# Seven block products in four instead of three of the eight K pairs of the gate and up matmuls

## The chip, the cores and the metric

The kernel runs on one core of a Trainium2 chip. The metric is the device time in microseconds (us) of one execution. Before the change its median over three runs is 2574.28 us (2572.94 to 2577.58).

## What is computed

A two-layer decoder trunk on 256 tokens of width 2048, in float32: layer 0 mixes with a state-space scan, layer 1 with differential attention, and each is followed by a SwiGLU feed-forward network (FFN) between RMSNorms. The change touches the FFN only:

```python
D_MODEL = 2048; SEQ = 256; D_FF = 5632; DEPTH = 2
def swiglu(h, w_gate, w_up, w_down):
    return (jax.nn.silu(h @ w_gate) * (h @ w_up)) @ w_down
...
for i in range(DEPTH):
    h = rmsnorm(x, norm_mix_pre[i])
    m = ssd_mixer(...) if i % 2 == 0 else diff_attention(...)
    x = x + rmsnorm(m, norm_mix_post[i])
    h = rmsnorm(x, norm_ffn_pre[i])
    x = x + rmsnorm(swiglu(h, ...), norm_ffn_post[i])
```

## The kernel before

**Numbers.** Every float32 matmul is done as three matmuls in TensorE's rounded type (float32r): an operand is split into a rounded part `hi` and a remainder `lo`, and hi·hi, hi·lo and lo·hi are summed in PSUM. The weights come from HBM as float32 into a tile `raw` of 128x4x512 (three buffers). `prep` (L112 to L126) makes `hi` on ScalarE (L119, a cast) and `lo` on VectorE (L120, raw minus hi). The `hi` and the `lo` tiles have four buffers each; a tile is given back when TensorE has used it. The activations lie transposed and split in `xT`.

**The FFN.** `ffn` works on 512-column chunks, 11 of gate and up. Chunk 10 goes through `mv` (eight ordinary products); the other ten go in five pairs through `pair` (L206 to L267), first gate, then up, so `pair` is called ten times in an FFN and twenty times in the kernel. The order is cut into three parts: chunks (10, 0, 1), then (2, 3, 4, 5), then (6, 7, 8, 9); behind each part `out_proj` multiplies what there is by w_down. So one part holds a gate and an up call, two parts hold gate, up, gate, up.

**One call of `pair`.** It multiplies two token tiles (t = 0, 1) by two column chunks over K = 2048. K is cut into eight pairs `kp` of two 128-row tiles, so that each `kp` is a product of a 2x2 block matrix (tokens by K halves) with a 2x2 block matrix (K halves by chunks). Two kinds of `kp` exist:

- an ordinary one (called R below): eight block products, 24 matmuls of 128x128 by 128x512, one `prep` of the four raw blocks (2048 elements per partition);
- one in `SEVEN` (called S below): seven block products, 21 matmuls, after the Winograd form of Strassen's scheme. A DMA on GpSimd's queue adds one weight block to another in SBUF (L233). `prep` of blocks 1 to 3 (1536 elements per partition) comes first; then VectorE makes three sums of weight blocks in place (L247 to L249, each reading what the one before wrote); then a second `prep` takes all four blocks (2048 elements). Four of the seven products (`p1`, `p5`, `p6`, `p7`) go to PSUM tiles `cp` that are summed over all S of the call and combined on VectorE at the last one (L263 to L267); the other three go straight to the accumulators `acc`.

An S also needs four sums of the activations of its K pair, the token forms. `make_form` (L754 to L768) computes them once per FFN and per S: six VectorE operations, a cast on ScalarE and a subtraction on VectorE, written to a tile `ff`. The first of them is put one step into the up product of chunk 10 and each next three steps later (`later(1 + 3 * k, ...)`, L804).

**The residual's places.** The tag `xr` has four buffers (L718). Outside the FFN's middle they hold the residual, two tiles for each token tile. Before the forms are made, the residual is written to DRAM (L802); before the last `out_proj` of the FFN it is fetched back (`fetch_x`, L721 to L728). In between the forms lie in those buffers: three of the four.

**Order.** The code emits a call `kp` by `kp`. Tile's planner makes one fixed order of instructions for each engine from it, and every engine works in that order; the `raw` loads go on SyncE's queue, the adding DMAs on GpSimd's. When the call's last `kp` is through, VectorE combines the accumulators with the saved products (L778 for gate, L787 and L788 for up), and for up the product is transposed by TensorE (L278) and split (L271 on ScalarE, L272 on VectorE).

Of the kernel before, what the change touches and what calls it, by code (L numbers as in the profile page):

```python
# [29 lines left out]
LAG = 4  # L30
LAG2 = 2

SEVEN = (2, 4, 6)


@with_exitstack
def trunk_kernel(ctx, tc, x_rows, x_cols, vec_cols, vec64, post_rows, lam_rows,
# [103 lines left out]
    def later(k, fn):  # L141
        at = step_no[0] + k
        i = len(deferred)
        while i and deferred[i - 1][0] > at:
            i -= 1
        deferred.insert(i, (at, fn))
# [592 lines left out]
    def ffn(wg, wu, wd, step, final):  # L739
# [14 lines left out]
        def make_form(kp):  # L754

            n, k = kp // 2, kp % 2 * 2
            xf = t512("xf", (P, NT, 2, P))
            f = t512("f", (P, 4, P))
            for t in range(NT):
                sl = slice(t * P, (t + 1) * P)  # L760
                nc.vector.tensor_tensor(xf[:, t], xT_hi[n][:, k:k + 2, sl].bitcast(F32),
                                        xT_lo[n][:, k:k + 2, sl].bitcast(F32), op=ALU.add)
            nc.vector.tensor_tensor(f[:, 0], xf[:, 1, 0], xf[:, 1, 1], op=ALU.subtract)
            nc.vector.tensor_tensor(f[:, 1], xf[:, 1, 0], xf[:, 0, 0], op=ALU.subtract)
            nc.vector.tensor_tensor(f[:, 2], xf[:, 0, 0], f[:, 0], op=ALU.subtract)
            nc.vector.tensor_tensor(f[:, 3], xf[:, 0, 1], f[:, 2], op=ALU.subtract)
            ff = forms[kp] = xr_tile("ff", (P, 4, 2, P), F32R)
            split(ff[:, :, 0], ff[:, :, 1], f)  # L768
# [5 lines left out]
        def g_done(p):  # L774
            def done(t, c, ps, ss):
                g, op = ss[(t, c)]
                gt[(t, 2 * p + 1 - c)] = g
                nc.vector.tensor_tensor(g, ps, g, op=op)  # L778
                nc.scalar.activation(g, g, AF.Silu, scale=rs(t))
            return done  # L780

        def u_done(p):
            def done(t, c, ps, ss):
                ch = 2 * p + 1 - c
                g = gt[(t, ch)]
                y, op = ss[(t, c)]
                nc.vector.tensor_tensor(y, ps, y, op=op)  # L787
                nc.vector.scalar_tensor_tensor(g, y, rs(t), g, op0=ALU.mult, op1=ALU.mult)  # L788

                def piece():  # L790
                    acts[(t, ch)] = act_piece(g, f"f{step}_{ch}_{t}")
                later(2, piece)
            return done

        def twos(w, c):
            return [[w[c + e, kp // 2, :, kp % 2 * 2:kp % 2 * 2 + 2] for e in range(2)] for kp in range(8)]

        mv([wg[10, k] for k in range(4)], u_stat, g_evac, LAG)
        for t in range(NT):
            rs(t)  # L800
            for h in range(2):
                nc.sync.dma_start(xr_d[t][h].rearrange("p (e k) -> p e k", e=2), xr_of[(t, h)])  # L802
        for k, kp in enumerate(SEVEN):
            later(1 + 3 * k, lambda kp=kp: make_form(kp))  # L804
        mv([wu[10, k] for k in range(4)], u_stat, u_evac, LAG2)
        parts = [(10, 0, 1), (2, 3, 4, 5), (6, 7, 8, 9)]
        for pi, part in enumerate(parts):
            for c in part:
                if c < 10 and c % 2 == 0:
                    pair(twos(wg, c), SEVEN, form, g_done(c // 2))  # L810
                    pair(twos(wu, c), SEVEN, form, u_done(c // 2))
            last = pi == len(parts) - 1
# [190 lines left out]
```

## Time and profile before

| | |
|---|---|
| median of 3 runs | 2574.28 us |
| the profiled execution | 2578.97 us, of it 2577.2 us span |
| TensorE granted clock | 0.997 |
| matmuls of `pair` (L224) | 3660, of 11922 in all |
| HBM read | 499.44 MB, 196 GB/s over the span |
| adding DMAs (L233) | 60 of 256 KB |

A row of a timeline gives the start, the duration, engine, line and operation, with how often it follows itself; in square brackets stands the idle time before it and what ended that. [...]

### The profile page before, as it was taken

The page shows a single profiled execution, that of the slowest core. Times are in us where ns is not written, and L with a number is a line of the kernel's source. Part 1 is how long each engine was busy: PE and PEld are TensorE (multiplying, and loading weights), DVE is VectorE, ACT ScalarE, POOL GpSimd, SP SyncE. Part 2 cuts the span into 40 slices and gives each one's busy share as a digit, 9 for nine tenths or more (in the row PEclk, how much of TensorE's full clock was granted, in tenths as well). Part 3 has the DMA queues.
Part 4 walks back from the last instruction along what each step waited for, and adds up shares of the span by engine and source line. Part 5 has one row for each costly group of instructions (what it writes and reads, how often), then busy time and mean ns, then how long its engine had stood idle before and what let it go on. Part 6 is the DMA issues. An engine that isn't in the chain of part 4 may idle for free.

```text
span 2577.2 us, 30784 instructions
## 1 busy us (share of the span) xinstructions
PE 2546.3 (99%) x11922; PEld 2082.6 (81%) x11922; DVE 1796.5 (70%) x2056; ACT 1335.3 (52%) x1628; POOL 204.5 (8%) x176
## 2 busy tenths in 40 slices
PE   8999999999999999999999999999999999999998
PEld 7877888788878888888888778887788888888886
DVE  8777547676677668856885665556578488758874
ACT  4676545665565454534454554445555455435542
POOL 2021000120100000000001000001100000000001
PEclk9999999999999999999999999999999999999999
DMA  6645555454756566666666544544566566656663
GB/s 222 205 166 188 180 193 196 167 180 164 269 200 212 212 198 210 210 215 197 205 235 229 190 147 164 170 157 143 211 198 228 199 208 206 224 194 206 208 243 132
DMA packets 120337, 507.80 MB, mean 197 GB/s; under 512 B 11840, under 2 KB 28544, under 8 KB 84352
## 3 DMA queue, kind: packets, MB, share of 16 engines
q1 hardware_dynamic: 110896, 489.27, 54.6%
q0 software_dynamic: 8640, 15.73, 3.8%
q8 instruction: 93, 1.52, 0.2%
q10 hardware_dynamic: 656, 0.85, 0.1%
q14 instruction: 52, 0.43, 0.1%
HBM read 499.44 MB, written 6.36 MB: 196 GB/s over the span
## 4 chain that ended last, share of the span: by engine, by line
PE 84%; DVE 7%; issue 4%; ACT 3%; DMA 3%; POOL 0%; DVEq 0%; SPq 0%; ACTq 0%; POOLq 0%
PE acc L173 49%; PE acc L224 19%; PE acc L198 5%; PE cp L224 5%; DVE lo L120 3%; PE acc L200 2%; ACT hi L119 2%; DMA raw<-in_w_u_dram 1%; PE sc L879 1%; DMA raw<-in_w_d_dram 1%; PE py L534 1%; PE pt_f L278 1%; DMA mt<-acum_d 1%; PE ptx L615 0%; PE pc L441 0%
## 5 line engine op out<-in xcount | busy, mean ns | idle before, releaser
L120 DVE TENSOR_TENSOR lo<-raw,hi 128x2048 fp32r<-128x2048 f32 (+2 forms) x548 | 1064.7, 1959 | 571.6 <-ACT hi L119 562.3
L119 ACT CAST hi<-raw 128x2048 fp32r<-128x2048 f32 (+2 forms) x548 | 877.1, 1612 | 877.0 <-PE acc L173 295.1
L173 PE MATMUL acc<-hi,xT 128*128 128x512 f32 x1792 | 591.5, 401 | 2.3 <-ACT xT L620 2.0
L224 PE MATMUL acc<-hi,xT 128*128 128x512 f32 x1840 | 589.1, 390 | 0.0
L224 PEld LDWEIGHTS acc<-hi,xT 128*128 128x128 f32 x1840 | 345.3, 188 | 71.2
L173 PEld LDWEIGHTS acc<-hi,xT 128*128 128x128 f32 x1792 | 337.0, 189 | 78.1 <-issue 5.9
L224 PE MATMUL acc<-lo,xT 128*128 128x512 f32 x920 | 358.1, 389 | 0.0
L173 PE MATMUL acc<-lo,xT 128*128 128x512 f32 x896 | 353.1, 394 | 1.6 <-DVE lo L120 1.6
L173 PE MATMUL acc<-hi,ah_f 128*128 128x512 f32 x704 | 274.5, 391 | 0.0
L173 PE MATMUL acc<-lo,ah_f 128*128 128x512 f32 x704 | 274.5, 390 | 0.0
L173 PE MATMUL acc<-hi,al_f 128*128 128x512 f32 x704 | 274.4, 390 | 0.0
L224 PEld LDWEIGHTS acc<-lo,xT 128*128 128x128 f32 x920 | 172.7, 188 | 36.2 <-DVE lo L120 0.4
L173 PEld LDWEIGHTS acc<-lo,xT 128*128 128x128 f32 x896 | 169.4, 189 | 38.4 <-issue 3.9
L198 PE MATMUL acc<-xT,hi 128*128 128x512 f32 x512 | 180.4, 398 | 0.0
L173 PEld LDWEIGHTS acc<-hi,al_f 128*128 128x128 f32 x704 | 132.2, 188 | 27.2
L173 PEld LDWEIGHTS acc<-lo,ah_f 128*128 128x128 f32 x704 | 132.2, 188 | 27.0 <-DVE lo L120 0.2
L173 PEld LDWEIGHTS acc<-hi,ah_f 128*128 128x128 f32 x704 | 132.2, 188 | 26.9
L200 PE MATMUL acc<-xT,lo 128*128 128x256 f32 x512 | 142.9, 280 | 0.0
L124 DVE SCALAR_TENSOR_TENSOR lo<-raw,cols,hi 128x512 fp32r<-128x512 f32 x128 | 92.6, 772 | 53.1 <-ACT hi L123 52.8
L224 PE MATMUL cp<-hi,ff 128*128 128x512 f32 x360 | 120.8, 390 | 0.0
L198 PEld LDWEIGHTS acc<-xT,hi 128*128 128x128 f32 x512 | 96.1, 188 | 23.0
L123 ACT ACTIVATE hi<-raw,cols 128x512 fp32r<-128x512 f32 x128 | 84.6, 715 | 53.1 <-PE acc L173 37.8
(247 smaller groups left out, 2844.1 us busy)
## 6 DMA issues: line engine op xcount, KB each, us to landing
raw<-in_w_d_dram SPq DMA_DIRECT2D x88, 1024.0 KB, 4.9
raw<-in_w_zxbc_dram SPq DMA_DIRECT2D x80, 1024.0 KB, 4.8
raw<-in_w_g_dram SPq DMA_DIRECT2D x160, 512.0 KB, 4.9
raw<-in_w_u_dram SPq DMA_DIRECT2D x160, 512.0 KB, 5.5
raw<-in_w_qkv_dram SPq DMA_DIRECT2D x48, 1024.0 KB, 4.8
raw<-in_w_so_dram SPq DMA_DIRECT2D x32, 1024.0 KB, 4.9
raw<-in_w_ao_dram SPq DMA_DIRECT2D x16, 1024.0 KB, 5.2
mt<-acum_d SPq DMA_DIRECT2D x16, 512.0 KB, 7.0
```

The source lines that it names most:

```text
L119: nc.scalar.copy(hi, raw)
L120: nc.vector.tensor_tensor(lo, raw, hi.bitcast(F32), op=ALU.subtract)
L123: nc.scalar.activation(hi[:, j], raw[:, j], AF.Copy, scale=scale[j])
L124: nc.vector.scalar_tensor_tensor(lo[:, j], raw[:, j], scale[j], hi[:, j].bitcast(F32), op0=ALU.mult, op1=ALU.subtract)
L173: nc.tensor.matmul(acc[t], a, b[:, j], start=(i == 0 and j == 0 and q == 0), stop=(i == last and j == 1 and q == 2))
L198: nc.tensor.matmul(acc[ct], hi[:, j, cs], x.rearrange("p a s -> p (a s)"), start=(i == 0 and j == 0), stop=False)
L200: nc.tensor.matmul(acc[ct][:, :S], lo[:, j, cs], x[:, 0], start=False, stop=(i == last and j == 1))
L224: nc.tensor.matmul(acc[k], a, b, start=first and q == 0, stop=last and q == 2)
L278: nc.tensor.transpose(pt[:, j], src[:, j * P:(j + 1) * P], ident)
L534: nc.tensor.matmul(py[e * 64:(e + 1) * 64, a], xd[c][:, 2 * a + e], mts[c][:, 2 * a + e], start=True, stop=True)
L879: nc.tensor.matmul(sc[c][:, h], qT[cp, h, ts], kT[cp, h, :nk * P], start=True, stop=True)
```

## The change

`SEVEN` names four K pairs instead of three, and other ones. `last` in `pair` stays K pair 6. A fourth form is made, at step 10, and the forms fill all four buffers of the tag `xr`.

```diff
-SEVEN = (2, 4, 6)
+SEVEN = (1, 3, 4, 6)
```

What reads it:

```python
for k, kp in enumerate(SEVEN):
    later(1 + 3 * k, lambda kp=kp: make_form(kp))
...
pair(twos(wg, c), SEVEN, form, g_done(c // 2))
pair(twos(wu, c), SEVEN, form, u_done(c // 2))
```

In a call the order of kinds was R R S R S R S R and is now R S R S S R S R.

## The prediction

> **What bounds the kernel now.** I read the page first, then the rows of one product tile on TensorE, then VectorE's timeline in a stretch of `pair`.
>
> ```profile
> span 2577.2 us, 30784 instructions
> PE   2546.3 (99%) x11922; PEld 2082.6 (81%) x11922; DVE 1796.5 (70%) x2056; ACT 1335.3 (52%) x1628; POOL 204.5 (8%) x176
> ```
> ```profile
> 776.55 0.39 PE L224 MATMUL cp<-hi,xT 128*128 128x512 f32 x1
> 786.75 0.39 PE L224 MATMUL cp<-hi,xT 128*128 128x512 f32 x1
> ```
>
> By the page TensorE (PE) is the bound and VectorE (DVE) has 30% to spare. Both numbers need care. The two rows are the first matmuls of K pair 2 and K pair 4 of one call: between them lie an S (21 matmuls) and an R (24), so 45 matmuls in 10.20 us, 0.2267 us each, not the 0.39 us that a row shows. An S costs TensorE 4.76 us, an R 5.44.
>
> The 70% is a mean over the whole kernel. In `pair` it is another matter. Here is VectorE in a gate call (all S work of it up to the combining, R means an L120 of 2048):
>
> ```profile
> 1264.10 1.75 DVE L120 TENSOR_TENSOR lo<-raw,hi 128x1536 fp32r<-128x1536 f32 x1
> 1265.89 0.69 DVE L247 TENSOR_TENSOR raw<-raw 128x512 f32<-128x512 f32 x1
> 1266.61 0.69 DVE L248 TENSOR_TENSOR raw<-raw 128x512 f32<-128x512 f32 x1
> 1267.22 0.68 DVE L249 TENSOR_TENSOR raw<-raw 128x512 f32<-128x512 f32 x1
> ...
> 1276.12 0.69 DVE L247 TENSOR_TENSOR raw<-raw 128x512 f32<-128x512 f32 x1
> ...
> 1286.45 0.69 DVE L247 TENSOR_TENSOR raw<-raw 128x512 f32<-128x512 f32 x1
> ...
> 1290.58 4.49 DVE L120 TENSOR_TENSOR lo<-raw,hi 128x2048 fp32r<-128x2048 f32 x2 [2.11 <-ACT hi L119]
> ```
> ```profile
> ACT hi L119 <- DVE raw L249: 224.7, 56, 5.8
> ```
>
> One S on VectorE is: `lo` of three blocks, three sums, then 2.11 us of nothing, then `lo` of four blocks. The hole is a dependency: ScalarE (ACT) can cast the sums only when the third is done, and VectorE can subtract only what is cast. The wait table has ScalarE waiting for L249 in 56 of the 60 S of the kernel, so almost no S is without it. From one L247 to the next is 10.33 us (1276.12 to 1286.45), an S and an R. Two `lo` of 2048 take 4.49 us, the first 2.29, so an R costs 2.20 and an S 8.13. TensorE does the same two in 10.20: VectorE's chain, holes included, is the slower one already.
>
> The rest of VectorE's work in a call is the combining. Two stretches, each with one R inside:
>
> ```profile
> 1210.10 0.68 DVE L264 TENSOR_TENSOR su<-cp,s 128x512 f32<-128x512 f32 x1
> 1214.08 2.28 DVE L120 TENSOR_TENSOR lo<-raw,hi 128x2048 fp32r<-128x2048 f32 x1
> 1217.48 1.75 DVE L120 TENSOR_TENSOR lo<-raw,hi 128x1536 fp32r<-128x1536 f32 x1
> ...
> 1251.58 0.68 DVE L264 TENSOR_TENSOR su<-cp,s 128x512 f32<-128x512 f32 x1
> 1260.70 2.28 DVE L120 TENSOR_TENSOR lo<-raw,hi 128x2048 fp32r<-128x2048 f32 x1
> ```
>
> After gate it takes 1217.48 − 1210.10 − 2.20 = 5.18 us, after up 1264.10 − 1251.58 − 2.20 = 10.32. So VectorE's chain is, for gate, 3 × 8.13 + 5 × 2.20 + 5.18 = 40.57 us, for up 45.71, together 86.28. TensorE's is 2 × 183 × 0.2267 = 82.97. From the first S to the last S of a part with four calls the chain gives 86.28 + 40.57 + (2 S and 2 R) 20.66 = 147.51 us. The first and the last `cp` of the two such parts of layer 0, and of the short part:
>
> ```profile
> L224 PE MATMUL cp<-hi,xT x24: 389/389/389, 926.6 to 1074.1; 128*128 128x512 f32 x24
> ```
> ```profile
> L224 PE MATMUL cp<-hi,xT x24: 389/389/389, 1185.3 to 1332.7; 128*128 128x512 f32 x24
> ```
> ```profile
> L224 PE MATMUL cp<-hi,xT x12: 389/389/389, 776.5 to 838.9; 128*128 128x512 f32 x12
> ```
>
> 147.5 and 147.4: TensorE and VectorE are level here, and TensorE hardly waits:
>
> ```profile
> PEld cp L224 <- DVE lo L120: 0.7, 3, 0.3
> ```
>
> That is in the stretch 1258 to 1301. TensorE is the bound by a hair, with VectorE on its heels.
>
> **The change, step by step.** *Removed:* three matmuls in each of 20 calls, 60 × 0.2267 = 13.6 us of TensorE, 0.5%. A call becomes 180 matmuls, 40.8 us.
>
> *Added on VectorE and ScalarE:* in each call one R becomes an S, 8.13 in place of 2.20 on VectorE's chain, +5.93 us (3.8 busy, 2.1 hole). On ScalarE a cast of three blocks more, which has room at 52%. The chain becomes 4 × 8.13 + 4 × 2.20 + 5.18 = 46.50 for gate, 51.64 for up, 98.1 for both, against 81.6 on TensorE. VectorE's chain is now the bound by far, and the saved matmuls are worth nothing there.
>
> How far can VectorE run ahead? Its lead is limited by the four `hi` tiles, which TensorE gives back. At one S of a call that starts level:
>
> ```profile
> 1203.30 6.88 DVE L120 TENSOR_TENSOR lo<-raw,hi 128x2048 fp32r<-128x2048 f32 x3 [2.11 <-ACT hi L119]
> ```
> ```profile
> 1205.69 0.39 PE L224 MATMUL cp<-hi,xT 128*128 128x512 f32 x1
> ```
>
> The sums' `lo` ends at 1203.30 + 2.29 = 1205.6, and TensorE needs it nine matmuls into the S, at 1207.7: 2.1 us of slack, once at the start of each part.
>
> Now the parts. From the first to the last `cp`, K pair 1 of the first call to K pair 6 of the last: in a part of two calls 46.50 + (3 S and 2 R) 28.79 = 75.3, in a part of four 98.14 + 46.50 + 28.79 = 173.4. Ahead of the first S there is one R less than before (−5.44); behind the last nothing changes. So a short part gains 75.3 − 62.4 − 5.4 − 2.1 = +5.4 us, a long one 173.4 − 147.5 − 5.4 − 2.1 = +18.4. Two FFNs with one short and two long each: 2 × (5.4 + 36.8) = +84 us.
>
> *What may fill holes:* four S in 20 calls make 80 holes of 2.11 us. Where the planner's fixed order puts combining work or the next cast between L249 and the second `lo`, a hole costs nothing. Bounds: none filled, 0; all filled, more than the whole loss. In before it fills hardly any (the wait row above), and where VectorE is tightest ScalarE stands still ahead of the sums' cast:
>
> ```profile
> 1267.98 5.10 ACT L119 CAST hi<-raw 128x2048 fp32r<-128x2048 f32 x3 [5.28 <-issue]
> ```
>
> Three casts in a row start here, the sums' first; the two behind it are of the next two K pairs and need no sums, yet none was put into the 5.28 us. I stay near that row. But the first S now comes right behind K pair 0, where the combining falls, so I let a quarter of 20 such holes be filled, −10 us. Sum: **+74 us**.
>
> *At nothing:* two more forms. One form is, from
>
> ```profile
> L761 DVE TENSOR_TENSOR xf<-xT x12: 416/419/423, 738.1 to 1881.3; 128x256 f32<-128x256 f32 x12
> L763 DVE TENSOR_TENSOR f<-xf x6: 285/292/294, 738.9 to 1884.6; 128x128 f32<-128x128 f32 x6
> L272 DVE TENSOR_TENSOR ff<-f,ff x6: 681/685/689, 742.2 to 1888.9; 128x512 fp32r<-128x512 f32 x6
> ```
>
> 2 × 0.42 + 4 × 0.29 + 0.69 = 2.7 us of VectorE. Cover is chunk 10's up product, where each K pair is an R and VectorE has holes such as
>
> ```profile
> 758.69 2.29 DVE L120 TENSOR_TENSOR lo<-raw,hi 128x2048 fp32r<-128x2048 f32 x1 [2.55 <-ACT hi L119]
> ```
>
> Uncovered, two would cost 5.4; nothing else of the change makes it less, so 0 to 5.4. The residual's first fetch found a free place and went early; now all four wait on SyncE's queue for forms, with weight loads behind them:
>
> ```profile
> SPq L725 <- PE cp L224: 3.3, 4, 1.1
> ```
>
> One more such wait per FFN is up to 1.1 us each, and the residual is needed only behind the last `out_proj`: 0 to 2.2, I take 0. K pairs 3 and 4 are neighbours, and an S holds its `raw` tile longest: load, adding DMA, sums, cast, `lo`.
>
> ```profile
> raw<-in_w_u_dram SPq DMA_DIRECT2D x160, 512.0 KB, 5.5
> raw<-in_w_u_dram POOLq DMA_DIRECT2D x30, 256.0 KB, 4.1
> ```
>
> With three tiles, the tile of K pair 3 is reloaded for 6, then for the next call's 1 and 4. From one release to the next takes 5.5 + 4.1 + three sums 2.0 + hole 2.1 + `lo` 2.2 = 15.9 us (GpSimd's issue apart). The chain above gives 2 × 8.13 + 2.20 = 18.5 for the same three K pairs, so the loads are covered, with 2.6 us to spare; their price is 0 here and comes up only if the chain is quicker.
>
> **The rivals.**
>
> *A, VectorE's chain binds in full* (the sum above): +45 to +100 us, about 2619 to 2674, chance 0.60.
>
> *B, the planner fills part of the holes.* In a chain that is behind, TensorE gives tiles back early, and the next K pair's cast could go ahead of the sums' cast. For: with K pairs 3 and 4 next to each other there is a cast of three blocks to put there. Against: it did not happen in before where VectorE was tight. With half of its 15 holes filled a long part has 15 × 1.05 us less, +2.6, and a short one is back at TensorE's bound, −6 × 0.2267 = −1.4: 4 × 2.6 − 2 × 1.4 = +8 in all. So +5 to +45, about 2579 to 2619, chance 0.17; within 5 us of before, chance 0.06. Here the three `raw` tiles would be next: a run of S in one tile, 3 to 6 to 1 to 4, is 3 × 15.9 = 47.7 for nine K pairs, in which TensorE needs 45.6.
>
> *C, TensorE stays the bound: faster.* If the holes are hidden, only busy time counts. In six calls of before VectorE is busy
>
> ```profile
> sum 251.10, PE 251.10 PEld 207.54 DVE 204.25 ACT 128.75 POOL 13.94; mean PE 41.85 PEld 34.59 DVE 34.04 ACT 21.46 POOL 2.32
> ```
>
> 34.04 of 41.85 us a call; 3.8 more are 37.9, below 40.8. Then the 13.6 us come in whole: 2560.7. It decides where more than about six in ten holes are filled. Chance 0.17. [...]
>
> **How the numbers follow.** The profiled execution took 2578.97 us, 0.2% over the median; the sum is a difference and I add it to the median: 2574.3 + 74 = 2648. About 0.2% (5 us) is what a measurement can tell from no change. Faster by more than that: C, 0.17. Within: 0.06. Slower: A and B, 0.77. The range leaves out C and what lies above A's end (few per cent): 2570 to 2675; A's own range is 2619 to 2674.
>
> **What would show it.** Right: 3600 matmuls on L224 with the same 0.2267 us between starts, waits of L224 for L120 that grow from a microsecond to some 70; 80 waits of about 2.1 us ahead of a 2048 `lo`; two L247 some 8.1 us apart in each call (K pairs 3 and 4); from first to last `cp` about 171 us in a long part, 73 in a short one. The step on the chain is wrong if L120's of 2048 follow L249 without a hole. Wrong altogether: a long part near 149 us from `cp` to `cp`, which is TensorE's bound there (3 × 40.8 + 25.2 = 147.6 of matmuls, and the transposes). If L247 waits for the adding DMA, the tiles of `raw` are what I priced too low.

## The result and the profile after

The changed kernel takes 2678.84 us (median of 4 runs, 2670.16 to 2682.77) against 2573.62 us of the kernel before on the same chip: ratio 1.0395 (95% interval 1.0383 to 1.0407), +105 us. The forecast was +74, with 2675 as the upper end: the direction was right, and the loss is larger than the range allowed. The profiled execution took 2681.9 us, 2680.1 of it span, at a granted clock of 0.987 (before 0.997).

The page of after, span and engines:

```profile
span 2680.1 us, 30843 instructions
PE 2581.8 (96%) x11862; PEld 2081.9 (78%) x11862; DVE 1871.1 (70%) x2150; ACT 1360.1 (51%) x1650; POOL 222.6 (8%) x196
```

VectorE has 75 us more to do, but its share of the span is 70%, as before. No share of this page shows what is wrong. VectorE's timeline in an up call of after does; its first two rows are the last of the gate call's combining and the first `lo` of K pair 1, the L247 are the first sums of K pairs 1, 3, 4 and 6:

```profile
1249.06 0.68 DVE L778 TENSOR_TENSOR sx<-acc,sx 128x512 f32<-128x512 f32 x1
1249.66 1.75 DVE L120 TENSOR_TENSOR lo<-raw,hi 128x1536 fp32r<-128x1536 f32 x1
1252.52 0.69 DVE L247 TENSOR_TENSOR raw<-raw 128x512 f32<-128x512 f32 x1 [1.11 <-DMA raw<-in_w_u_dram]
...
1262.85 0.69 DVE L247 TENSOR_TENSOR raw<-raw 128x512 f32<-128x512 f32 x1
...
1264.18 0.69 DVE L249 TENSOR_TENSOR raw<-raw 128x512 f32<-128x512 f32 x1
1266.97 3.96 DVE L120 TENSOR_TENSOR lo<-raw,hi 128x2048 fp32r<-128x2048 f32 x2 [2.11 <-ACT hi L119]
1270.97 0.69 DVE L247 TENSOR_TENSOR raw<-raw 128x512 f32<-128x512 f32 x1
...
1281.29 0.69 DVE L247 TENSOR_TENSOR raw<-raw 128x512 f32<-128x512 f32 x1
```

K pairs 3 and 4 stand 8.12 us apart (forecast 8.13), an S and an R 10.32 (forecast 10.33), and the 2.11 us hole is there. From the table of waits of after:

```profile
ACT hi L119 <- DVE raw L249: 352.5, 72, 6.6
PE cp L224 <- ACT hi L119: 47.6, 28, 3.4
PE acc L224 <- ACT hi L119: 19.2, 40, 0.6
DVE raw L247 <- DMA raw<-in_w_u_dram: 20.4, 12, 4.0
```

The columns are total us, times, longest. ScalarE now waits for the third sum in 72 of 80 S; in VectorE's timeline of the whole kernel the hole behind it is 2.0 to 2.1 us long in 79 of the 80. And L224 waits 47.6 + 19.2 = 66.8 us (forecast some 70, though named for L120; it is the cast, L119, that the first product with summed blocks lacks). The last line is what the forecast had priced at nothing: the first sum waits 20.4 us for the adding DMA; in before that wait is

```profile
DVE raw L247 <- DMA raw<-in_w_u_dram: 1.9, 3, 1.1
```

From the first to the last `cp`, the short part and the two long parts of layer 0 of after:

```profile
L224 PE MATMUL cp<-hi,xT x16: 389/389/389, 772.9 to 850.0; 128*128 128x512 f32 x16
```
```profile
L224 PE MATMUL cp<-hi,xT x32: 389/389/393, 933.4 to 1106.6; 128*128 128x512 f32 x32
```
```profile
L224 PE MATMUL cp<-hi,xT x32: 389/389/393, 1212.1 to 1388.3; 128*128 128x512 f32 x32
```

77.1, 173.2 and 176.2 us, where the forecast had 73 and 171; in layer 1 they are 74.4, 172.0 and 172.3. All but 2 us of the loss of the two profiled executions (101.3 of 103.0) lies in the six parts that call `pair`; `out_proj`, the mixers and chunk 10 are as long as before.

One wait for the adding DMA, close up. GpSimd's and then VectorE's timeline of after, around K pair 1 of an up call:

```profile
1344.41 0.88 POOL L233 DMA_DIRECT2D raw<-in_w_u_dram  x1 [18.35 <-DVE sw L265]
```
```profile
1336.40 4.58 DVE L120 TENSOR_TENSOR lo<-raw,hi 128x2048 fp32r<-128x2048 f32 x2 [2.11 <-ACT hi L119]
...
1352.24 0.69 DVE L247 TENSOR_TENSOR raw<-raw 128x512 f32<-128x512 f32 x1 [2.60 <-DMA raw<-in_w_u_dram]
```

The tile's last reader is the sums' `lo` of the S before, the first of the two that start at 1336.40 (done at about 1338.7). Behind the tile's load the adding DMA is issued at 1344.4, and the sum that reads it starts at 1352.2, 7.8 us later. The forecast had put in 4.1 us, the median from issue to landing. Its first packet moved at 1348.75, by the trace. Ahead of it SyncE had issued two weight loads for other tiles, from 1341.02 and from 1343.82; the first had landed by then (1347.75), the second had not (1351.39).

The place is typical. Of the 20.4 us, 18.8 fall on K pair 1 of the ten up calls, the rest on K pair 4. At K pair 1 of an up call all ten adding DMAs took 7.0 to 9.0 us from issue to landing, 7.6 in the median; at K pairs 3 and 6 the medians are 4.1 and 4.0.

### The profile page after: what moved, and what is told of

Its sections match the earlier page's. It is cut to its first block, busy times and chain, and to the rows that moved or that the text cites. A ratio compares the mean times of both kernels' runs of the same rounds, so it can differ in the third digit from the quotient of the medians.

```text
span 2680.1 us, 30843 instructions
## 1 busy us (share of the span) xinstructions
PE 2581.8 (96%) x11862; PEld 2081.9 (78%) x11862; DVE 1871.1 (70%) x2150; ACT 1360.1 (51%) x1650; POOL 222.6 (8%) x196
## 4 chain that ended last, share of the span: by engine, by line
PE 61%; DVE 17%; issue 8%; ACT 7%; DMA 6%; POOL 0%; ACTq 0%; DVEq 0%; SPq 0%; POOLq 0%
PE acc L173 46%; DVE lo L120 7%; ACT hi L119 6%; DMA raw<-in_w_u_dram 6%; PE acc L198 4%; PE acc L224 3%; PE acc L200 2%; DVE raw L247 2%; DVE raw L248 2%; DVE raw L249 1%; PE sc L879 1%; PE cp L224 1%; DVE al_f L272 1%; PE py L534 1%; PE ptx L615 0%
## 5 line engine op out<-in xcount | busy, mean ns | idle before, releaser
L120 DVE TENSOR_TENSOR lo<-raw,hi 128x2048 fp32r<-128x2048 f32 (+2 forms) x568 | 1098.9, 1951 | 587.0 <-ACT hi L119 578.8
L119 ACT CAST hi<-raw 128x2048 fp32r<-128x2048 f32 (+2 forms) x568 | 901.6, 1606 | 932.5 <-DVE raw L249 352.5
L173 PE MATMUL acc<-hi,xT 128*128 128x512 f32 x1792 | 592.1, 401 | 2.3 <-ACT xT L620 1.9
L224 PE MATMUL acc<-hi,xT 128*128 128x512 f32 x1600 | 542.5, 399 | 19.2 <-ACT hi L119 19.2
L173 PEld LDWEIGHTS acc<-hi,xT 128*128 128x128 f32 x1792 | 337.6, 189 | 78.4 <-issue 5.9
L224 PEld LDWEIGHTS acc<-hi,xT 128*128 128x128 f32 x1600 | 302.3, 191 | 98.5 <-ACT hi L119 37.8
L173 PE MATMUL acc<-lo,xT 128*128 128x512 f32 x896 | 353.6, 395 | 1.4 <-DVE lo L120 1.4
L224 PE MATMUL acc<-lo,xT 128*128 128x512 f32 x800 | 312.9, 391 | 0.0
L224 PE MATMUL cp<-hi,ff 128*128 128x512 f32 x480 | 171.9, 413 | 47.6 <-ACT hi L119 47.6
L173 PEld LDWEIGHTS acc<-lo,xT 128*128 128x128 f32 x896 | 169.7, 189 | 37.9 <-issue 3.9
L224 PEld LDWEIGHTS acc<-lo,xT 128*128 128x128 f32 x800 | 151.1, 189 | 33.4 <-DVE lo L120 0.5
L224 PEld LDWEIGHTS cp<-hi,ff 128*128 128x128 f32 x480 | 92.7, 198 | 78.0 <-ACT hi L119 59.4
```

The lines of the kernel that those rows point to most:

```text
L119: nc.scalar.copy(hi, raw)
L120: nc.vector.tensor_tensor(lo, raw, hi.bitcast(F32), op=ALU.subtract)
L173: nc.tensor.matmul(acc[t], a, b[:, j], start=(i == 0 and j == 0 and q == 0), stop=(i == last and j == 1 and q == 2))
L224: nc.tensor.matmul(acc[k], a, b, start=first and q == 0, stop=last and q == 2)
```

## The experiments

**Theory 1**: the hole of 2.11 us in each S makes VectorE's chain the bound, and the rest (adding DMA, forms, residual) is small. **Theory 2**: the three `raw` tiles, with load, adding DMA and sums in a row, are the bound or the next one. **Theory 3**: the forms and the residual's places cost time. All runs stand against the kernel before on the same chip (2575.8 to 2576.4 us).

### Was TensorE the bound before?

*Three matmuls less, nothing else.* The kernel before; in each call K pair 1 leaves out one block product.

```diff
                     for j in range(2):
+                        if kp == 1 and (t, c, j) == (1, 1, 1):
+                            continue
                         mm((t, c), x_stat(2 * kp + j, t), hi[:, e + j], lo[:, e + j], kp == end and j == 1)
```

> Before with three matmuls of K pair 1 left out in every call (one block product missing, so the output is not the reference's): what the change saves on TensorE, without what it adds on VectorE. If TensorE alone bound the kernel, 60 x 0.2267 = 13.6 us come in: about 2560. Theory 1 with VectorE level before the change: gate and up have 86.3 us of chain against then 81.6 of TensorE, the parts of four calls stay at about 147 from first to last cp, and less than half comes in: 2567 to 2574.

2563.62 us, ratio 0.9961 (0.9947 to 0.9975): by the medians −12.2 of the 13.6 us that the matmuls cost, by the interval −6 to −14. The second long part of layer 0 of this kernel:

```profile
L224 PE MATMUL cp<-hi,xT x24: 389/389/389, 1179.1 to 1324.8; 128*128 128x512 f32 x24
```

145.7 us in place of 147.4, with VectorE's work unchanged; the two of layer 1 are 145.7 and 146.0, the first of layer 0 stays at 147.3. So TensorE did bound the kernel before, and the chain stood some 2 us per long part below it, not level with it. That part of the forecast was drawn too tight.

*The kernel before with the hole cut.* The second cast and its `lo` in two halves, the first of them behind the second sum. The same edit comes again below:

```diff
+            i = seq[0]
+            seq[0] += 1
+            sh = hl[0].tile([P, 4, 512], F32R, tag="hi", name=f"hi{i}")
+            sl = hl[0].tile([P, 4, 512], F32R, tag="lo", name=f"lo{i}")
             nc.vector.tensor_tensor(raw[:, 2], raw[:, 2], raw[:, 0], op=ALU.add)
             nc.vector.tensor_tensor(raw[:, 3], raw[:, 3], raw[:, 2], op=ALU.add)
+            nc.scalar.copy(sh[:, 2:4], raw[:, 2:4])
             nc.vector.tensor_tensor(raw[:, 1], raw[:, 2], raw[:, 1], op=ALU.subtract)
-            sh, sl = prep(raw)
+            nc.scalar.copy(sh[:, 0:2], raw[:, 0:2])
+            for e in (2, 0):
+                nc.vector.tensor_tensor(sl[:, e:e + 2], raw[:, e:e + 2], sh[:, e:e + 2].bitcast(F32), op=ALU.subtract)
```

> The kernel before (K pairs 2, 4, 6) with the second cast and remainder in two halves. Theory (the dependency hole decides, VectorE's chain binds wherever it is longer than TensorE's): the hole falls from 2.11 to some 1.0 us, the chain of a gate and an up call from 86.3 to some 80, TensorE with 83.0 is the bound, so little is to be had: 2568 to 2577, and the waits of L224 stay near nothing. Rival (before was bound by VectorE's chain): the 60 holes are worth 1.1 us each, 2505 to 2540.

2575.70 us, ratio 1.0001 (0.9992 to 1.0010). The half `lo` waits for its cast 34.5 us in all here, 0.58 in the mean of the 60 S in place of 2.11: sixty shorter holes buy nothing where TensorE is the bound.

### The forms and the residual's places

*A fourth form in the kernel before*, in the residual's fourth place, and a copy of one column of it into a new 4-byte tile at the end, so that its place stays taken:

```diff
-        for k, kp in enumerate(SEVEN):
+        for k, kp in enumerate(SEVEN + (1,)):
...
+                touch = small.tile([P, 1], F32, tag="touch", name="touch", bufs=1)
+                nc.scalar.copy(touch, forms[1][:, 0, 0, 0:1].bitcast(F32))
```

> Before with three S, and a fourth form (of K pair 1) made as in the change and held in the fourth place of the residual until the last part's out_proj, where one element of it is copied. No product uses it. It is the forms' part of the change alone. Theory 1: it costs nothing, 2570 to 2582. Rival (the residual's places and the fourth form cost): 10 us or more, above 2585.

2602.70 us, ratio 1.0103 (1.0086 to 1.0120), a miss. But the matmuls themselves had changed, and the first `cp` came 9 us later (785.7 in place of 776.5). The short part's `cp` row of this kernel, and two groups of L224:

```profile
L224 PE MATMUL cp<-hi,xT x12: 396/396/397, 785.7 to 849.5; 128*128 128x512 f32 x12
```
```profile
L224 PE MATMUL acc<-hi,xT 128*128 128x512 f32 x1840 | 600.1, 395 | 0.0
L224 PE MATMUL acc<-hi,ff 128*128 128x512 f32 x120 | 46.7, 389 | 0.0
```

No matmul waits, those against `ff` take 389 ns as before, those against `xT` 394 to 396 in the mean, in place of 389 to 390. A call has 147 of them: at 5 to 7 ns each 0.7 to 1.0 us, and twenty calls alone are some 15 to 20 us of the 26. Something other than the forms was slow. *So again, with the column copied into a tile that is there already:*

```diff
-                touch = small.tile([P, 1], F32, tag="touch", name="touch", bufs=1)
-                nc.scalar.copy(touch, forms[1][:, 0, 0, 0:1].bitcast(F32))
+                nc.scalar.copy(table, forms[1][:, 0, 0, 0:1].bitcast(F32))
```

> The kernel before with a fourth form made, in the residual's fourth place and held to the end of the gate and up part by a copy of one column into a tile that exists already, so that no tile moves in SBUF. Theory (forms and places cost next to nothing, and the 1.0% of the earlier version came from the moved tiles): matmuls of the pair calls at 0.2267 us again, 2573 to 2582. Rival (the fourth form and the lost early fetch are the cost): 2595 to 2605 as in the earlier version.

2575.28 us, ratio 1.0002 (0.9994 to 1.0011). The same row:

```profile
L224 PE MATMUL cp<-hi,xT x12: 389/389/389, 776.5 to 838.8; 128*128 128x512 f32 x12
```

A fourth form and its place cost nothing; theory 3 is out.

### The hole

*The kernel after with the halves* (the edit shown above):

> The changed kernel with the second cast of each S in two halves, blocks 2 and 3 behind the second sum and blocks 0 and 1 behind the third, and the lo in the same two halves: less cut up than the four casts, which the planner had mixed with casts of other K pairs. If the planner keeps the halves together, the hole shrinks from 2.1 to some 0.7 us and theory 1 gives 2580 to 2640. If it puts other casts in between again, ScalarE's order makes VectorE wait elsewhere, and it is 2670 or more; then nothing follows for the theory.

2588.20 us, ratio 1.0047 (1.0032 to 1.0062): of +105 us +12 are left. VectorE's timeline of this kernel, K pairs 3, 4 and 6 of a call (L251 is the first sum here, L254 the third, L257 the half `lo`):

```profile
1224.93 0.69 DVE L251 TENSOR_TENSOR raw<-raw 128x512 f32<-128x512 f32 x1
...
1227.54 2.36 DVE L257 TENSOR_TENSOR lo<-raw,hi 128x1024 fp32r<-128x1024 f32 x2 [0.59 <-ACT hi L253]
...
1231.67 0.69 DVE L251 TENSOR_TENSOR raw<-raw 128x512 f32<-128x512 f32 x1
...
1241.05 0.69 DVE L251 TENSOR_TENSOR raw<-raw 128x512 f32<-128x512 f32 x1
```
```profile
DVE raw L251 <- DMA raw<-in_w_u_dram: 2.8, 4, 1.3
```

The hole is 0.59 us, an S costs 6.74, an S and an R 9.38. Put into the prediction's own sum: a part of four calls is 2 × 4 × 9.38 + 5.18 + 10.32 + (4 × 9.38 + 5.18) + (2 × 9.38 + 6.74) = 158.7 us from first to last `cp`, a part of two 68.2. So 158.7 − 147.5 − 5.4 − 2.1 = +3.7 and 68.2 − 62.4 − 5.4 − 2.1 = −1.7, and over the kernel 4 × 3.7 − 2 × 1.7 = +11. Measured: +12 by the medians, +7 between the two profiled executions. The wait for the adding DMA went down from 20.4 us to 2.8 with it.

*The third sum on GpSimd, besides.* 

```diff
-            nc.vector.tensor_tensor(raw[:, 1], raw[:, 2], raw[:, 1], op=ALU.subtract)
+            nc.gpsimd.tensor_tensor(raw[:, 1], raw[:, 2], raw[:, 1], op=ALU.subtract)
```

> The kernel after with the halves, and the third of the three sums on GpSimd, beside VectorE's and ScalarE's work. Theory (VectorE's chain is the bound): VectorE loses 0.65 us per S, but GpSimd takes 1.3 to 1.9 us for a sum of this size, so the second half's cast comes later and the hole takes back what the sum gave: 2580 to 2600, near the 2588 of the halves alone. Rival (VectorE's busy time is what counts): 80 x 0.65 us off the part where it binds, 2560 to 2575.

2672.39 us, ratio 1.0375 (1.0362 to 1.0388): above both expectations. ScalarE's timeline, VectorE's, and the group of the sum:

```profile
1229.26 1.05 ACT L255 CAST hi<-raw 128x1024 fp32r<-128x1024 f32 x1 [5.25 <-POOL raw L254]
1230.21 1.05 ACT L253 CAST hi<-raw 128x1024 fp32r<-128x1024 f32 x1
```
```profile
1230.34 2.36 DVE L257 TENSOR_TENSOR lo<-raw,hi 128x1024 fp32r<-128x1024 f32 x2 [2.26 <-ACT hi L255]
```
```profile
L254 POOL TENSOR_TENSOR raw<-raw 128x512 f32<-128x512 f32 x80 | 136.5, 1706 | 317.6 <-DVE raw L251 207.3 <-issue 102.7 <-ACT sw L786 5.3
```

The planner put the half that needs GpSimd's sum (L255) ahead of the one that was ready (L253). The hole is 2.26 us again, 1.67 more than with the halves alone, and the sum that left VectorE was worth some 0.65 (the three take 2.0): 80 × (1.67 − 0.65) = 82 us, and 84 were measured. Its first sums wait 4.1 us for the adding DMA, so a late adding DMA is not the reason. VectorE had less to do and the kernel was slower: the hole, not the work, sets the time.

*The second cast in four*, each part behind its sum, `lo` in two:

```diff
...
+            nc.scalar.copy(sh[:, 0], raw[:, 0])
             nc.vector.tensor_tensor(raw[:, 2], raw[:, 2], raw[:, 0], op=ALU.add)
+            nc.scalar.copy(sh[:, 2], raw[:, 2])
...
-            sh, sl = prep(raw)
+            nc.scalar.copy(sh[:, 1], raw[:, 1])
...
```

> The changed kernel with the second cast of each S cut into four, one behind each sum, and the second lo cut in two, the blocks that are ready first ahead. The work is the same and a little more; only the hole between L249 and the lo should go. Theory 1: an S falls from 8.13 to 6.0 to 6.4 us, gate and up to 82 to 85 us against 81.6 of TensorE, so the loss goes: 2560 to 2590. Rival 1 (the amount of work on VectorE binds, not the hole): no more than 10 us less than the changed kernel, about 2670 or, with the extra operations, slower. Rival 2 (the adding DMAs and the three raw tiles bind): 2640 to 2670, with the idle time moving to L247 waiting for the DMA.

2703.85 us, ratio 1.0500 (1.0481 to 1.0519), a miss. ScalarE's timeline of this kernel, then VectorE's (L253, L255 and L257 are the casts behind the three sums L252, L254 and L256, L259 the half `lo`):

```profile
1261.40 1.89 ACT L119 CAST hi<-raw 128x2048 fp32r<-128x2048 f32 x1
1263.20 0.71 ACT L788 ACTIVATE su<-su,rs_pre 128x512 f32<-128x512 f32 x1
1263.81 0.70 ACT L788 ACTIVATE sx<-sx,rs_pre 128x512 f32<-128x512 f32 x1
1264.43 0.60 ACT L253 CAST hi<-raw 128x512 fp32r<-128x512 f32 x1
```
```profile
1260.89 0.68 DVE L256 TENSOR_TENSOR raw<-raw 128x512 f32<-128x512 f32 x1
1265.58 2.36 DVE L259 TENSOR_TENSOR lo<-raw,hi 128x1024 fp32r<-128x1024 f32 x2 [4.00 <-ACT hi L255]
```

The planner put another K pair's cast and two scalings ahead of the small casts, and the hole is 4.00 us here. That is one of the longest: in the whole kernel the half `lo` waits for a small cast 125.2 us in 62 places, less than the holes of after (167 us). What rose is the first sum's wait for the adding DMA, 43.7 us in place of 20.4. So cutting finer is no cure by itself, but which of the two makes the loss was not tried.

*The sums behind the second cast and its `lo`*, so that nothing waits for them (the last four products then use blocks that are not summed):

```diff
+            sh, sl = prep(raw)
             nc.vector.tensor_tensor(raw[:, 2], raw[:, 2], raw[:, 0], op=ALU.add)
             nc.vector.tensor_tensor(raw[:, 3], raw[:, 3], raw[:, 2], op=ALU.add)
             nc.vector.tensor_tensor(raw[:, 1], raw[:, 2], raw[:, 1], op=ALU.subtract)
-            sh, sl = prep(raw)
```

> The changed kernel with the three sums of each S moved behind the second cast and its lo (the sums then reach no matmul, so the output is not the reference's). Every operation of VectorE, ScalarE, TensorE and the DMAs is still there; only the dependency cast-on-sums is gone, and with it the hole of 2.11 us. Theory 1 (the chain with its hole binds): an S costs VectorE 6.0 us instead of 8.13, gate and up 81 us against 81.6 of TensorE, most of the loss goes: 2570 to 2610. Rival 1 (VectorE's busy time binds): within 20 us of the changed kernel, above 2655. Rival 2 (load, adding DMA and three raw tiles bind as soon as the chain is shorter): 2610 to 2655, with VectorE and ScalarE waiting for DMAs.

2629.29 us, ratio 1.0205 (1.0190 to 1.0220): half of the loss stays, in theory 2's band. The waits of ScalarE for weights of this kernel, in after 39.1 and 10.3 us:

```profile
ACT hi L119 <- DMA raw<-in_w_u_dram: 192.4, 74, 6.2
ACT hi L119 <- DMA raw<-in_w_g_dram: 111.7, 43, 5.6
```

By these waits the `raw` tiles are the next limit without the hole. This order is worse for them than the halves, where the same waits are 24.8 and 9.9 us: the sums are the tile's last use, and the planner lets them trail behind other `lo`.

### The adding DMA and the neighbours

*The kernel after without the adding DMA* (the sums then run on a block to which nothing was added):

```diff
-            if kp in seven:
-                nc.gpsimd.dma_start(raw[:, 0:1], src[0][:, 1:2], accum_op=ALU.add)
```

> The changed kernel without the adding DMA on GpSimd's queue (the first block of each S lacks one addend, so the output is not the reference's). Theory 1: only the 20 us go that L247 waited for the DMA, 2650 to 2665. Rival (the long stay of an S in its raw tile binds): more than half of the loss goes, below 2625.

2660.47 us, ratio 1.0330 (1.0315 to 1.0346): +85 in place of +105, and from the two profiled executions 18 us less. The short part and the first long part of this kernel:

```profile
L224 PE MATMUL cp<-hi,xT x16: 389/389/389, 771.3 to 842.5; 128*128 128x512 f32 x16
```
```profile
L224 PE MATMUL cp<-hi,xT x32: 389/389/395, 925.9 to 1096.9; 128*128 128x512 f32 x32
```

71.2 and 171.0 us (the second long part 171.0 too; in layer 1 72.8, 169.6 and 173.9), and +84.7 us in all: the chain's sum of the prediction ahead of its deduction for filled holes, 171 and +84. Some 18 to 20 us of the loss are the adding DMA. They lie where the waits do: from the first sum of K pair 6 of a gate call to that of K pair 1 of the up call it takes 19.0 us in after and 17.3 here (medians of ten), and ten times 1.7 us are 17.

*Three S with K pairs 3 and 4 side by side:*

```diff
-SEVEN = (2, 4, 6)
+SEVEN = (3, 4, 6)
```

> Before with K pairs (3, 4, 6) instead of (2, 4, 6): three S as before, but two of them neighbours, as in the changed kernel. Theory 1 (what binds is the sum of VectorE's chain, 8.13 us for each S with its 2.11 us hole and 2.20 for each R): the sum is that of before, 86.3 us for a gate and an up call, so within about 15 us of before, 2570 to 2590. Rival (the neighbours do it: two S in a row outrun the lead, and TensorE does not get the time back): half or more of the 105 us, above 2620.

2592.02 us, ratio 1.0068 (1.0053 to 1.0083): above theory 1's band, far below its rival's. No matmul was saved or added; two neighbours alone cost 16 us. Its wait for the adding DMA is

```profile
DVE raw L247 <- DMA raw<-in_w_u_dram: 14.4, 10, 3.1
```

all ten at K pair 3 of an up call. That it makes the 16 us is not shown: TensorE's own waits for VectorE and ScalarE in L224 add up to 4.9 us, the tile of K pair 3 held an ordinary K pair before, and this order was not run without the adding DMA.

*Four S, every other K pair:*

```diff
-SEVEN = (1, 3, 4, 6)
+SEVEN = (0, 2, 4, 6)
```

> The changed kernel with the four S at K pairs 0, 2, 4, 6: none has a neighbour. Theory 1: the sum of VectorE's chain is the same, so the loss is nearly the same: 2650 to 2700. Rival (the neighbours 3 and 4 make the loss): below 2615.

2637.35 us, ratio 1.0233 (1.0218 to 1.0249): +61, between the expectations. Its wait for the adding DMA is

```profile
DVE raw L247 <- DMA raw<-in_w_u_dram: 3.9, 2, 2.4
```

which takes most of the 20 us away; 24 more are gone against +85. The larger share of them is the place of the first S of a part. It stands one K pair earlier, so one R less lies ahead of it at TensorE's pace, 5.44 us, and one more in VectorE's chain, 2.20. The prediction's own sum for this order is therefore 6 × 3.24 = 19 us lower, +65 and not +84, which the expectation overlooked. The short part and the first long part of this kernel:

```profile
L224 PE MATMUL cp<-hi,xT x16: 389/389/476, 769.2 to 840.8; 128*128 128x512 f32 x16
```
```profile
L224 PE MATMUL cp<-hi,xT x32: 389/389/478, 918.7 to 1089.6; 128*128 128x512 f32 x32
```

From the last `cp` of the one to the first of the other lie 77.9 us, without the adding DMA 83.4, in before 87.7. Over the kernel the stretches outside of first to last `cp` are 56 us shorter than in before, those without the adding DMA 30.

With K pair 0 an S, the combining of the call before also falls among its sums, and a part of some holes is filled. VectorE's timeline of this kernel, in one of the places where much is filled:

```profile
1230.80 0.68 DVE L249 TENSOR_TENSOR raw<-raw 128x512 f32<-128x512 f32 x1
1231.40 0.68 DVE L778 TENSOR_TENSOR su<-acc,su 128x512 f32<-128x512 f32 x1
1232.00 0.68 DVE L778 TENSOR_TENSOR sx<-acc,sx 128x512 f32<-128x512 f32 x1
1233.58 2.29 DVE L120 TENSOR_TENSOR lo<-raw,hi 128x2048 fp32r<-128x2048 f32 x1 [0.90 <-ACT hi L119]
1236.61 3.96 DVE L120 TENSOR_TENSOR lo<-raw,hi 128x2048 fp32r<-128x2048 f32 x2 [0.74 <-ACT hi L119]
```

Here 1.2 of the 2.1 us are filled, and 0.74 come back ahead of the next `lo`. Eight of the 20 S at K pair 0 keep the whole hole. All 80 holes add up to 158 us, in after to 167: filling is worth at most some 9 us, and 65 − 9 + 4 = 60, where 61 were measured. So the filling that the prediction had allowed for does happen in this place, but it is small.

*The same four with the halves.* It was to join what both had won.

> Four K pairs 0, 2, 4, 6, every one with an ordinary one behind it, and the second cast and remainder in two halves. Theory: neither the hole nor the neighbours in one raw tile are left; the chain is still 4 x 9.4 + 5.2 = 42.8 us for gate and 47.9 for up against 40.8 on TensorE, part of the combining going into holes: a gain of at most the 13.6 us against the kernel before is not reached, 2565 to 2585. Rival (with the hole and the wait for the adding DMA gone TensorE is the bound): 2560 to 2564.

2611.08 us, ratio 1.0137 (1.0124 to 1.0150): a miss, 23 us slower than the halves with K pairs 1, 3, 4, 6. The first sum's group of this kernel:

```profile
L251 DVE TENSOR_TENSOR raw<-raw 128x512 f32<-128x512 f32 x80 | 55.2, 690 | 33.9 <-DMA raw<-in_w_u_dram 25.3 <-DMA raw<-in_w_g_dram 6.9
```

With the chain quicker the adding DMA is late again, by 32.2 us. One such place, in SyncE's and then VectorE's timeline of this kernel:

```profile
1228.46 11.40 SPq L230 DMA_DIRECT2D raw<-in_w_u_dram  x8
```
```profile
1226.16 2.28 DVE L120 TENSOR_TENSOR lo<-raw,hi 128x2048 fp32r<-128x2048 f32 x1
1228.36 1.22 DVE L257 TENSOR_TENSOR lo<-raw,hi 128x1024 fp32r<-128x1024 f32 x1
...
1243.10 0.69 DVE L251 TENSOR_TENSOR raw<-raw 128x512 f32<-128x512 f32 x1 [2.40 <-DMA raw<-in_w_u_dram]
```

The combining, mixed in with K pair 0's sums, holds its tile until 1229.6, and K pair 1's until 1228.4; only then do the next loads start, close behind each other, and K pair 4's first sum waits for the last of them and its adding DMA. That this is the cause in all 16 waits was not tried. No version that does the whole work beats the kernel before.

## Why the prediction was right and where it was wrong

**Right: what binds.** Rival A's chain is what the trace shows, S at 8.12 us and S plus R at 10.32. The 13.6 us of TensorE are worth nothing in after; cutting the hole in halves gives some 90 us of the 105 back (a wait for the adding DMA that is 17.6 us shorter among them), and the prediction's own sum, with the halves' distances put in, gives +11 where +12 was measured. Rival C (busy time counts, 2560.7) fell: in after VectorE is busy for 70% of the span, TensorE for 96%, and still it is VectorE's chain that binds. Rival B (the planner fills the holes) fell as well: 79 of 80 holes are whole.

**Wrong: "the loads are covered, with 2.6 us to spare; their price is 0".** This is the step that put the time outside of the range. The sum of 15.9 us for a tile used the median landing of an adding DMA, 4.1 us, and was held against K pairs 4 to 6, where the chain gives 18.5. The tightest place is another: from K pair 6 of a gate call to K pair 1 of the up call, in one tile, the chain has two R, the combining and an S, 2 × 2.20 + 5.18 + 8.13 = 17.7 us. And there the adding DMA took 7.6 us in the median, which makes the tile's sum 15.9 + 3.5 = 19.4; the trace has 19.0, and 17.3 without that DMA. The price was 18 to 20 us, from the kernel without it. Why its landing is longer at this place is not shown; in the instance above its first packet moved 4.3 us after the issue, with one of two loads for other tiles, issued ahead of it, landed and the other under way. The prediction named the sign to look for (L247 waiting for the adding DMA), but gave the cost no upper bound.

**Wrong: "I let a quarter of 20 such holes be filled, −10 us".** None was: with K pair 0 an ordinary one the combining is over (1249.06) before the first S makes its sums (1252.52), so it has no hole to fill, and 171.0 us per long part without the adding DMA is the chain with every hole in it. 84 + 18 = 102 of the 105 us are then accounted for. The remainder of 3 us is below the 5 us that a measurement can tell from nothing.

**Too tight: "level".** In before TensorE was the bound with some room: 12.2 of 13.6 us came in when matmuls alone were taken away, and shorter holes changed nothing. That the chain's 147.51 met the measured 147.5 was chance: the sum for after takes 2.1 us of slack off each part, that for before did not, and with it the chain of before is 145.4; the 145.7 to which a long part falls with fewer matmuls leaves room for that, 147.5 does not fit it. That did not hurt the forecast, which used the measured 147.5 us of before, but "level" gave TensorE's matmuls too little worth there.

**Right at nothing:** the fourth form and the residual's fetch, 1.0002 (0.9994 to 1.0011).

## What to carry to other kernels

Count an engine's chain with its dependency holes, from one repeat to the next, before comparing it with another engine's busy time: a saved matmul is worth something only while that chain is the shorter one. A transfer that "just fits" between two uses of a buffer needs its price taken at the place where the time is shortest, not from the median over all places (7.6 us there against 4.1), and needs an upper bound of its own. When two orders of the same work are compared, what lies ahead of the first slow step counts too: with K pairs 0, 2, 4, 6 it was worth more than the holes that were filled. Cut a hole by giving the waiting engine its input earlier, and look at the order on the other engine afterwards: a cast in two parts brought some 90 us back, in four it cost 25 more.

## What was not expected of the hardware

With one 4-byte tile more in SBUF, and no matmul waiting, L224's matmuls against `xT` lasted 394 to 396 ns in the mean, in place of 389 to 390, those against `ff` 389 to 390, and the kernel was 1.0% slower; without that tile the time was that of before (ratio 1.0002), and the `cp` row at 389 ns again. That the tile moved `xT` or other tiles in SBUF, and that this is the cause, was the author's guess from these two kernels; no run shows it. Whoever adds a small tile for an experiment should look at the matmul's duration first.

The granted clock was lower in the kernels in which TensorE waited for tens of us. L224's waits for other engines add up to 68.7 us in after, at a clock of 0.987; to 68.5 with the cast in four, at 0.985; to 6.8 with the halves, at 0.997; in before it has none, at 0.997. In after's trace the longest of these waits, 3.4 us, ends at 820.3 us, and the clock is 0.52 between 820.3 and 823.7, 1.00 in the 7 us ahead of 820 and in the 7 us behind 824.

Neither the longest wait nor the sum puts the kernels in the order of their clocks. Without the adding DMA the clock was 0.988, the waits of L224 sum to 54.5 us, and TensorE's longest wait in that whole kernel was 2.9 us:

```profile
PE cp L224 <- ACT hi L119: 35.3, 18, 2.9
```

With the third sum on GpSimd it was 0.992, with 62.2 us in all and no wait above 2.4 us. How the clock depends on the waits is not shown. It cost little: without the adding DMA the long parts of layer 0 came to the chain's 171.0 us all the same, since the chain that bound them was not TensorE's.
